# Hybrid decoder trunk on one core: residual loaded into the sum's tiles, mLSTM tiles in stages, S5 output products tied behind a later product

## The chip, the cores and the metric

The kernel runs on one core of a Trainium2 chip. The metric is the device time of one execution in microseconds, from the start to the end on the chip; each kernel is run several times, and the median is compared. A core has the engines TensorE (PE, matmuls; its weight loads are listed apart as PEld), VectorE (DVE), ScalarE (ACT), GpSimd (POOL) and SyncE (SP), which here only issues DMAs. Each engine and each DMA queue works through its own list of instructions in order and waits where a semaphore tells it to.

## The reference

One layer of a recurrent decoder trunk, run for a prompt of 2048 tokens with 16 learned meta tokens ahead of it, and for 8 sample sequences of 8 tokens. D_MODEL is 1024; three branches of width 512 are fed by one combined projection and gated into the sum.

```
h = rms_norm(x, norm_w)
proj = h @ w_in                        # q,k,v of two branches, S5 input, gates
qkv = causal_conv(conv_buf, dn_qkv)    # DeltaNet: short conv, l2 norms, delta rule in chunks
o_dn = rms_norm(delta_rule(q, k, v, g, beta)) * silu(dn_z)
o_ml = rms_norm(mlstm(q, k, v, ig, lf)) * sigmoid(ml_o) * silu(ml_z)   # matrix memory (c, n, m)
y5 = gelu(s5(s5_u));  y5 = y5 * sigmoid(y5 @ w_glu + b_glu);  o_s5 = y5 * silu(s5_z)
mixed = gates[0] * (o_dn @ w_branch_dn) + gates[1] * (o_ml @ w_branch_ml) + gates[2] * (o_s5 @ w_branch_s5)
x = x + mixed @ w_out
y = rms_norm(x, final_norm_w)
```

The outputs are y for both groups and all recurrent states.

## The kernel before

Tokens run in six blocks of (2, 3, 3, 3, 3, 2) tiles of 128; the first block also has the 80 sample and meta tokens. Activations stand with features on the partitions and the block's tokens T (336, then 384, at last 256) along the free dimension.

A product (`product`, `mm` at L195) is one 128 x T tile of output. fp32 is made of two halves: for each k the weight tile w (128 x 512, four k at once, 256 KB, DMA on SP's queue, L221) is cast to wh on ACT (L222) and VectorE subtracts wl = w - wh (L184), and three matmuls wh xh, wh xl, wl xh go into one of three PSUM banks named pd. Products with 8 k have 24 matmuls; those of the branch outputs (`wb`) and of `wg` have 12. Three buffers each hold wh and wl. So TensorE follows a stream of weights, ACT and VectorE prepare it, and in between they evict finished products and do the branches' own work.

What a block does is listed in a string of steps (`PLAN`, `PLAN0` for the first block): u and s are the S5 projections and scans, d and m the DeltaNet and mLSTM projections (numbers 8 to 11 are the v heads), M the mLSTM tiles (`ml_tile`), F the S5 finish, N the mLSTM output (`ml_out`, by `finish`), inv and D the DeltaNet inverse and tiles, E its output (also by `finish`), X2, X1 and X0 the gated branch sums (`mix`). After the steps come the next block's `norm` and this block's `out`. The code is recorded in that order; a scheduler in the framework then settles each engine's order from it, from priorities and from its own guesses of durations.

`norm` loads x in eight rows (xt, L329, SP's queue), sums squares (nacc, nsq), has a matmul that spreads the reciprocal root (`pr<-nsq,c`), scales xt in place on VectorE, casts it to xh on ACT (L357) and leaves xl to POOL. `out` does eight products of mh and ml with `wo`. For each it loads the residual row into a temporary ox on ACT's queue (L1320), and VectorE evicts with h = 0.5 pd + ox (L192). Then come the squares of h, the last norm, and the store of h (L1329, ACT's queue).

`ml_tile` for one tile: spread and exp (mlew, mldd), qk on TensorE, q * ew on POOL (`ml<-ml,mlew`), transposes of k and v (`tok`, `tr` at L199), kw = k * wst on VectorE, va = v on ACT (L894) with a column of ones set by POOL (L895), then the products with the state (`pr<-c,ml`) and with the tile (`pr<-va,mldd`). The DeltaNet's matrix P is scaled on POOL (`P<-P,dnx`, and `P<-P,ff` in `finish`). `s5_scan` has input products, a scan on VectorE and POOL (s5a), and output products (`s<-s5a,s5w`).

Of the kernel before, what the change touches and what calls it, by code (L numbers as in the profile page):

```python
# [38 lines left out]
PLAN0 = ("m8 m7 R m6 m10 m1 m0 m9 m2 m4 m5 d4 m3 d5 m11 M d0 d3 d2 S d7 d8 d9 d10 d1 d6 pre inv d11 N X1 D "  # L39
         "F X2 Ud E X0 Um").split()  # L40
PLAN = ("u0 u1 u2 u3 s0 s1 s2 s3 d0 d1 m1 m0 m2 m3 d6 d2 d10 d3 m4 m7 m6 d7 d4 d5 m5 d8 pre d9 m9 d11 m11 m10 m8 M F N inv D X2 "
        "X1 E X0").split()
# [10 lines left out]
    "macc": "wide", "ox": "wide", "rb": "wide", "s5v": "raw", "s5g": "wide", "raw": "raw", "junk": "junk",  # L53
# [49 lines left out]
class Kernel:  # L103
# [123 lines left out]
    def product(self, src, nk, xh, xl, T, lead=None):  # L227
# [4 lines left out]
        for k in range(nk):  # L232
# [4 lines left out]
            self.mm(o, l[:, k % 4], xh(k), start=False, stop=k == nk - 1)  # L237
# [11 lines left out]
    def setup(self):  # L249
# [41 lines left out]
        self.s_i = self.c_i = 0  # L291


    def block(self, b):
        self.b = b
# [16 lines left out]
        self.us = self.us_d[b % 2]  # L312
        self.ys = self.ys_d[b % 2]
        self.dn, self.ml, self.br, self.cst, self.acc = [None] * 3, [None] * 3, [None] * 3, None, None

        self.segs = ([(0, 8, 8), (NS, 1, NM)] if self.first else []) + [(self.p0, BLOCKS[b], P)]

    def norm(self):

        T, V = self.T, self.V  # L320
        xu = [self.unit([P, 4, T], name="xt") for _ in range(2)]
        xt = [xu[k // 4][:, k % 4] for k in range(8)]
        for k in range(8):
            src = self.I["xt"][k, :, self.t0:self.t0 + T]
            if self.first:
# [6 lines left out]
        if self.first:  # L332
# [11 lines left out]
        with self.tc.high_priority(offset=5000 if self.first else 0):  # L344
            rb = self.rstd_row(acc)
        xh, xl = ([self.xp.tile([P, 4, TMAX], F32R, name=self.name(s), tag=s, bufs=2)[:, :, :T] for _ in range(2)]
                  for s in ("xh", "xl"))
        if self.first:
            self.rb = self.temp([P, TMAX], "rb")[:, :T]
            self.A.copy(self.rb, rb)  # L350
            self.xh, self.xl, self.xn = uh, ul, (xh, xl)
        else:
            self.xh, self.xl = xh, xl
        with self.tc.high_priority(offset=3000 if self.first else 0):
            for k in range(8):
                self.stt(xt[k], xt[k], w(k), rb, OP.mult, OP.mult)
                self.A.copy(xh[k // 4][:, k % 4], xt[k])  # L357
                self.tt(V if self.first and k < 4 else self.G, xl[k // 4][:, k % 4], xt[k], xh[k // 4][:, k % 4], OP.subtract)
# [4 lines left out]
    def add_square(self, acc, x, first):  # L363
        if first:
            self.act(acc, x, AF.Square)
        else:
            sq = self.temp([P, TMAX], "nsq")[:, :self.T]
# [3 lines left out]
    def rstd_row(self, acc):  # L371

        T, V, nt = self.T, self.V, self.nt
        pc = self.ps([P, nt])
# [1150 lines left out]
```

## Time and profile before

| | us |
|---|---|
| median of three runs | 2824.74 |
| lowest and highest of the three | 2822.19, 2829.98 |
| the profiled execution, its own time | 2815.57 |
| its span, first to last instruction | 2813.8 |
| TensorE busy in the span | 2657.2 |
| TensorE's mean granted clock | 0.975 |

The profiled execution is one more execution, with the profiler on; its time lies 9.2 us below the median, and 1.8 us of it lie outside the span. Times of trace rows count from the start of the span. The granted clock is a share of full speed (2.4 GHz); 0.50 is the lower level, 1.2 GHz. A matmul's row gives the time to its modelled end; consecutive matmuls overlap, so their spacing is read from the starts.

### The profile page before, as it was taken

The numbers are of one execution on the slowest core, as the hardware profiler recorded it, in microseconds if no ns is written. First come the engines' busy times: TensorE is split into PE (matmuls) and PEld (weight loads), VectorE is DVE, ScalarE is ACT, GpSimd is POOL, SyncE is SP. The second block draws the span as 40 slices with busy tenths as digits, with TensorE's granted clock in tenths as the row PEclk, the third lists the DMA queues.
The fourth block names the chain that finished last, engine by engine and source line by source line (L and its number), as shares of the span: only waits on it lengthen the run. The fifth ranks groups of instructions, "written<-read, shape, count | busy, mean of one in ns | idle before, by whom it ended". The sixth has DMA issues, their size and how long they took to land.

```text
span 2813.8 us, 49701 instructions
## 1 busy us (share of the span) xinstructions
PE 2657.2 (94%) x17416; PEld 2579.1 (92%) x17416; DVE 2049.5 (73%) x4386; ACT 1256.8 (45%) x2855; POOL 759.0 (27%) x917
## 2 busy tenths in 40 slices
PE   6898999989999999999999999999999999988998
PEld 5898898989999989899999989999899999988998
DVE  8888766788764587885568788456888745689865
ACT  4353343534533444553344454344445434445544
POOL 7642333222302312321230241123123012113022
PEclk8998999999999999999999999999999999999999
DMA  5544546555343455433345533335554434564545
GB/s 153 164 151 143 162 137 200 181 161 158 104 123 102 140 179 159 136 109 115 107 147 169 172 118 120 107 114 156 168 162 116 130 94 126 155 201 144 174 136 154
DMA packets 303290, 404.24 MB, mean 144 GB/s; under 512 B 109472, under 2 KB 138912, under 8 KB 303040
## 3 DMA queue, kind: packets, MB, share of 16 engines
q1 hardware_dynamic: 283248, 374.73, 44.6%
q10 hardware_dynamic: 19792, 26.34, 2.8%
q8 instruction: 137, 2.24, 0.3%
q14 instruction: 113, 0.93, 0.1%
HBM read 369.42 MB, written 31.53 MB: 142 GB/s over the span
## 4 chain that ended last, share of the span: by engine, by line
PE 80%; DVE 11%; POOL 3%; DMA 2%; issue 2%; ACT 1%; SPq 0%; DVEq 0%; ACTq 0%; POOLq 0%
PE pd L195 66%; PE pr L195 9%; PE s L195 3%; DVE wl L184 2%; PE pr L199 2%; DVE s5a L1205 1%; POOL s5a L184 1%; DMA ox<-in_xt_dram 1%; DVE h L192 1%; DVE s5a L184 1%; DVE cacc L192 1%; DMA w<-in_wi_dram 1%; POOL P L184 1%; POOL s5xy L184 0%; ACT xh L357 0%
## 5 line engine op out<-in xcount | busy, mean ns | idle before, releaser
L222 ACT CAST wh<-w 128x512 fp32r<-128x512 f32 x1092 | 673.9, 619 | 990.5 <-PE pd L195 828.5
L184 DVE TENSOR_TENSOR wl<-w,wh 128x512 fp32r<-128x512 f32 x1092 | 812.7, 746 | 407.1 <-ACT wh L222 393.4
L195 PE MATMUL pd<-xh,wh 128*128 128x384 f32 (+2 forms) x3272 | 1078.7, 330 | 28.5 <-DVE cacc L192 16.8
L195 PE MATMUL pd<-xh,wl 128*128 128x384 f32 (+2 forms) x3272 | 1078.7, 330 | 17.5 <-DVE wl L184 17.0
L195 PE MATMUL pd<-xl,wh 128*128 128x384 f32 (+2 forms) x3272 | 1070.4, 327 | 9.4 <-DVE xl L184 9.4
L195 PEld LDWEIGHTS pd<-xh,wh 128*128 128x128 f32 x3272 | 625.5, 191 | 36.0 <-issue 8.4
L195 PEld LDWEIGHTS pd<-xh,wl 128*128 128x128 f32 x3272 | 624.4, 191 | 34.1 <-DVE wl L184 28.3
L195 PEld LDWEIGHTS pd<-xl,wh 128*128 128x128 f32 x3272 | 625.7, 191 | 11.8 <-DVE xl L184 9.8
L184 POOL TENSOR_TENSOR macc<-macc,mt 128x384 f32<-128x384 f32 (+2 forms) x96 | 124.7, 1299 | 389.0 <-DVE mt L192 382.3
L184 POOL TENSOR_TENSOR s5a<-s5a,s5a 128x384 f32<-128x384 f32 (+2 forms) x72 | 76.9, 1075 | 555.4 <-DVE s5a L184 522.6
L195 PE MATMUL pd<-mh,wh 128*128 128x384 f32 (+2 forms) x384 | 126.5, 331 | 11.6 <-ACT xh L357 7.0
L195 PE MATMUL pd<-mh,wl 128*128 128x384 f32 (+2 forms) x384 | 126.3, 331 | 3.9 <-DVE wl L184 3.6
L195 PE MATMUL pd<-ml,wh 128*128 128x384 f32 (+2 forms) x384 | 125.9, 329 | 0.0
L192 DVE SCALAR_TENSOR_TENSOR cacc<-pd,c,cacc 128x384 f32<-128x384 f32 (+1 forms) x180 | 103.9, 582 | 2.8 <-ACT cacc L181 1.5
L192 DVE SCALAR_TENSOR_TENSOR mt<-mt,pd 128x384 f32<-128x384 f32 (+2 forms) x96 | 50.1, 522 | 73.5 <-PE pd L195 73.1
L195 PE MATMUL s<-s5U,s5w 128*128 128x96 f32 (+2 forms) x576 | 86.0, 278 | 14.9 <-issue 9.2
L178 POOL COPY U<-UC 32x128 f32<-32x128 f32 x68 | 21.7, 337 | 290.5 <-DMA UC<-scru 289.2
L195 PEld LDWEIGHTS s<-s5U,s5w 128*128 128x128 f32 x576 | 79.3, 197 | 16.0 <-issue 15.5
L184 POOL TENSOR_TENSOR s5a<-s5a,s5t 128x384 f32<-128x384 f32 (+2 forms) x48 | 69.5, 1447 | 72.7 <-issue 32.7
L195 PEld LDWEIGHTS pd<-mh,wh 128*128 128x128 f32 x384 | 74.2, 193 | 14.6 <-ACT xh L357 13.0
L181 ACT ACTIVATE mt<-pd,c 128x384 f32<-128x384 f32 (+2 forms) x144 | 79.4, 551 | 0.4
L195 PEld LDWEIGHTS pd<-mh,wl 128*128 128x128 f32 x384 | 74.2, 193 | 5.9 <-DVE wl L184 5.8
(399 smaller groups left out, 4476.5 us busy)
## 6 DMA issues: line engine op xcount, KB each, us to landing
w<-in_wi_dram SPq DMA_DIRECT2D x816, 256.0 KB
w<-in_wb_dram SPq DMA_DIRECT2D x144, 256.0 KB
s5w<-s5w SPq DMA_DIRECT2D x120, 256.0 KB
w<-in_wo_dram SPq DMA_DIRECT2D x96, 256.0 KB
s5t<-s5p SPq DMA_DIRECT2D x48, 192.0 KB
w<-in_wg_dram SPq DMA_DIRECT2D x24, 256.0 KB
xt<-in_xt_dram SPq DMA_DIRECT2D x32, 192.0 KB
ox<-in_xt_dram ACTq DMA_DIRECT2D x32, 192.0 KB
```

Source lines behind the costliest of these rows:

```text
L178: return eng.tensor_copy(out, in_)
L181: return self.A.activation(out, in_, f, **k)
L184: return eng.tensor_tensor(out, a, b, op=op)
L192: return self.V.scalar_tensor_tensor(out, a, s, b, op0=op0, op1=op1)
L195: return self.E.matmul(out, lhsT, rhs, start=start, stop=stop, **k)
L199: return self.E.transpose(out, in_, self.ident[:n, :n])
L222: self.A.copy(h, w)
L1205: V.tensor_tensor_scan(g[:, a, 1:1 + m], self.s5R[:, 4 * f + a:4 * f + a + 1].to_broadcast([P, m]), x[:, a, 0:m], g[:, a, 0:1], OP.mult, O ...
```

## The change

There are five edits.

1. `out` allots its two tiles h (128 x 4 x T each) first and loads the residual straight into them with two DMAs on SP's queue; the eviction works in place. The temporaries ox and their eight loads on ACT's queue go.
2. Steps are generators that can be advanced by stages: a plan word `w:n` runs n stages of it, the bare word the rest. `ml_tile` has stages (spread to q * ew; kw and a small copy ec; v copy and its ones column; the products). `M0:2` stands ahead of m11 and `M1:2` ahead of m10, so that two tiles' first stages are recorded ahead of the last v projections (m11, m10, m8). The ones column is copied on ACT from a constant, and C * ec reads the small copy.
3. In the S5 scans the output products are a second stage; a word with `!` is tied by `issue_after` behind the last matmul of the product recorded last, without a semaphore. They are recorded after the next scan's input stage and two projections.
4. `finish` records the gate of head h ahead of the transposes of head h - 1.
5. `norm`, `out`, the DeltaNet tiles and `dn_pre` are written as generators too; `OUT` has all stages of norm ahead of those of out, as before, and the merge `dn_merge` is a step g of its own ahead of each D.

```diff
-PLAN = ("u0 u1 u2 u3 s0 s1 s2 s3 d0 d1 m1 m0 m2 m3 d6 d2 d10 d3 m4 m7 m6 d7 d4 d5 m5 d8 pre d9 m9 d11 m11 m10 m8 M F N inv D X2 "
-        "X1 E X0").split()
+OUT0 = ["n"] * 19 + ["o"] * 99
+PLAN = ("R C u0 u1 u2 u3 s0:1 s1:1 d0 d1 s0! s2:1 m1 m0 s1! s3:1 m2 m3 s2! d6 d2 s3! d10 d3 m4 m7 m6 d7 d4 d5 m5 d8 p d9 m9 "
+        "d11 M0:2 m11 M1:2 m10 m8 M0 M1 M2 F N I g0 D0 g1 D1 g2 D2 X2 X1 E X0").split()
+OUT = ["n"] * 19 + ["o"] * 99
...
-            self.mm(o, l[:, k % 4], xh(k), start=False, stop=k == nk - 1)
+            self.tail = self.mm(o, l[:, k % 4], xh(k), start=False, stop=k == nk - 1).ins
...
-        for h in range(4):
-            z = gate(h)
-            p = self.ps([P, T])
-            for i, (o, n) in enumerate(self.tiles):
-                self.tr(p[:, o:o + n], raw[:n, i, h])
+        z = [None] * 4
+        for h in range(5):
+            yield
+            if h < 4:
+                z[h] = gate(h)
+            if h:
+                p = self.ps([P, T])
+                for i, (o, n) in enumerate(self.tiles):
+                    self.tr(p[:, o:o + n], raw[:n, i, h - 1])
...
         self.tt(G, q[:, :, o:o + n], q[:, :, o:o + n], ew, OP.mult)
+        yield
...
         self.tt(V, kw[:n], self.tok(k, o, n), self.b4(self.wst, i, n), OP.mult)
+            ec = self.small([P, 4, 1], "mlec")
+            A.copy(ec, ew[:, :, n - 1:n])
+        yield
         A.copy(va[:n, :, 0:P], self.tok(v, o, n))
-        G.memset(va[:n, :, P:P + 1], 1.0)
+        A.copy(va[:n, :, P:P + 1], self.ones[:n, 0:4][:, :, None])
+        yield
...
-            self.tt(G, Cn, C, ew[:, :, n - 1:n].to_broadcast([P, 4, 129]), OP.mult)
+            self.tt(G, Cn, C, ec.to_broadcast([P, 4, 129]), OP.mult)
...
                     self.tt(V, x, x, y, op)
                     self.tt(V, out[j], x, bv[j][:, :, :, l], OP.add)
+        yield
         yp = self.ps([P, 4, n], "s5")
...
-    def out(self):
-        V, A, G, T = self.V, self.A, self.G, self.T
+    def out(self, g, mh, ml):
+        V, A, G, T = self.V, self.A, self.G, g.T
+
         hu = [self.unit([P, 4, T], name="h") for _ in range(2)]
+        for k in range(2):
+            self.nc.sync.dma_start(hu[k], self.I["xt"][4 * k:4 * k + 4, :, g.t0:g.t0 + T].rearrange("k p t -> p k t"))
         acc = self.temp([P, TMAX], "nacc")[:, :T]
         for d in range(8):
-            x = self.temp([P, TMAX], "ox")[:, :T]
-            self.nc.scalar.dma_start(x, self.I["xt"][d, :, self.t0:self.t0 + T])
             h = hu[d // 4][:, d % 4]
             with self.tc.high_priority(offset=WPRIO):
-                self.stt(h, ps, 0.5, x, OP.mult, OP.add)
+                self.stt(h, ps, 0.5, h, OP.mult, OP.add)
...
+            for w in PLAN0 if self.first else PLAN:
+                late = w[-1] == "!"
+                w, _, n = w.rstrip("!").partition(":")
+                if w[0] in "gMD" and int(w[1:]) >= self.nt:
+                    continue
+                with self.tc.issue_after(self.tail) if late else nullcontext():
+                    self.advance(w, steps, int(n) if n else -1)
```

How the edits move instructions is seen in the order that the scheduler makes. The first place is VectorE in the output stage of the fourth block. Names: wl is a weight's lower half, rs_t, nr and nsq are norm's reciprocal roots, xt norm's rows, h the sum's tile, pd a finished product, ox a residual row. Before:

```order
L184 TENSOR_TENSOR wl_21689<-w_21687,wh_21688 128x512
L192 SCALAR_TENSOR_TENSOR rs_t_21492<-nr_21489 128x3
L184 TENSOR_TENSOR rs_t_21492<-rs_t_21492,nvar_21488 128x3
L192 SCALAR_TENSOR_TENSOR nr_21489<-rs_t_21492,nr_21489 128x3
L188 TENSOR_SCALAR nsq_21504<-c_92,nr_21489 128x128 x3
L184 TENSOR_TENSOR wl_21714<-w_21712,wh_21713 128x512
L192 SCALAR_TENSOR_TENSOR xt_21451<-xt_21451,c_91,pr_21508 128x384 x3
L192 SCALAR_TENSOR_TENSOR h_21538<-pd_21541,ox_21578 128x384
L192 SCALAR_TENSOR_TENSOR xt_21451<-xt_21451,c_91,pr_21508 128x384
L192 SCALAR_TENSOR_TENSOR xt_21452<-xt_21452,c_91,pr_21508 128x384 x4
```

The same place of the changed kernel, with the start of norm's chain:

```order
L188 TENSOR_TENSOR wl_21606<-w_21604,wh_21605 128x512
L196 SCALAR_TENSOR_TENSOR h_21518<-pd_21523,h_21518 128x384
L188 TENSOR_TENSOR wl_21624<-w_21622,wh_21623 128x512
L196 SCALAR_TENSOR_TENSOR h_21518<-pd_21562,h_21518 128x384
L188 TENSOR_TENSOR wl_21647<-w_21645,wh_21646 128x512
L193 TENSOR_SCALAR nvar_21468<-pr_21464 128x3
```

And its end:

```order
L192 TENSOR_SCALAR nsq_21484<-c_92,nr_21469 128x128 x3
L196 SCALAR_TENSOR_TENSOR h_21518<-pd_21603,h_21518 128x384
L188 TENSOR_TENSOR wl_21688<-w_21686,wh_21687 128x512
L188 TENSOR_TENSOR nacc_21522<-nacc_21522,nsq_21600 128x384
L188 TENSOR_TENSOR nacc_21522<-nacc_21522,nsq_21641 128x384
L188 TENSOR_TENSOR wl_21706<-w_21704,wh_21705 128x512
L196 SCALAR_TENSOR_TENSOR xt_21431<-xt_21431,c_91,pr_21488 128x384 x3
L196 SCALAR_TENSOR_TENSOR h_21518<-pd_21644,h_21518 128x384
```

The first eviction stood behind the chain and behind three rows of xt; now two evictions stand ahead of the chain, the third behind nsq, and the fourth behind three rows of xt. On TensorE `pr<-nsq,c` stood at the end of the third product of `wo` and stands near the end of the fourth. On SP's queue the two loads of h follow norm's loads and stand among the first weights of `wo`: one h, a weight, the other h.

The second place is POOL around the mLSTM tiles of the fourth block. P and dn are the DeltaNet's, c_119 and c_120 the mLSTM state, ml q, s5g the S5 finish. Before:

```order
L184 TENSOR_TENSOR c_120<-c_119,mlew_18498 128x516
L184 TENSOR_TENSOR s5g_18689<-s5g_18689,s5g_18685 128x384
L184 TENSOR_TENSOR P_18121<-P_18121,dnx_18213 128x512 x3
L184 TENSOR_TENSOR s5g_18702<-s5g_18702,s5g_18698 128x384
L184 TENSOR_TENSOR ml_17756<-ml_17756,mlew_18498 128x4x128
L895 MEMSET va_18578 128x4
```

Now:

```order
L188 TENSOR_TENSOR c_120<-c_119,mlec_18383 128x516
L188 TENSOR_TENSOR ml_17730<-ml_17730,mlew_18358 128x4x128
L188 TENSOR_TENSOR s5g_18669<-s5g_18669,s5g_18665 128x384
L188 TENSOR_TENSOR ml_17730<-ml_17730,mlew_18425 128x4x128
L188 TENSOR_TENSOR s5g_18682<-s5g_18682,s5g_18678 128x384
L188 TENSOR_TENSOR P_18095<-P_18095,dnx_18187 128x512 x3
```

The q products of two tiles went ahead of the three P, and the memset is gone.

The third place is TensorE at the same tiles, at the end of the last v projection (pd); va is v with its ones, mldd the weights in the tile. Before:

```order
L195 MATMUL pd_18457<-xh_16316,wl_18478 128x384
L195 MATMUL pr_18508<-ml_17756,ml_17413 128x128 x4
L199 MATMUL pr_18517<-c_92,ml_17413 128x128 x4
L199 MATMUL pr_18523<-c_92,ml_18295 128x128 x4
L195 MATMUL pr_18531<-c_119,ml_17756 128x129
L195 MATMUL pr_18531<-va_18516,mldd_18502 128x129
```

Now:

```order
L199 MATMUL pd_18490<-xh_16304,wl_18511 128x384
L203 MATMUL pr_18528<-c_92,ml_18269 128x128 x4
L199 MATMUL pr_18536<-c_119,ml_17730 128x129
L199 MATMUL pr_18543<-c_119,ml_17730 128x129
L199 MATMUL pr_18536<-va_18376,mldd_18362 128x129
```

qk and the transposes of k (the first two rows behind pd before) went ahead, into the projections before this one; the transposes of v stay. Elsewhere on TensorE the S5 output products stand in whole groups of twelve inside later products, and the transposes of the DeltaNet's finish stand 18 matmuls ahead of the first branch product, where they stood 55 ahead.

## Rows read from the trace of the kernel before

**Rows 1.** The page, busy time of each engine and the chain that ended last

```profile
PE 2657.2 (94%) x17416; PEld 2579.1 (92%) x17416; DVE 2049.5 (73%) x4386; ACT 1256.8 (45%) x2855; POOL 759.0 (27%) x917
...
PE 80%; DVE 11%; POOL 3%; DMA 2%; issue 2%; ACT 1%; SPq 0%; DVEq 0%; ACTq 0%; POOLq 0%
```

**Rows 2.** Windows, one steady block: busy us (x count), granted clock, DMA share, GB/s

```profile
1930.00:2405.00 475.00, 459.71 (x2902) 450.82 (x2901) 337.24 (x698) 212.22 (x476) 111.15 (x110) 0.99 0.45 135
```

**Rows 3.** TensorE's waits: us in total, times, longest us

```profile
PE pd L195 <- DVE wl L184: 21.6, 28, 2.7
...
PE pr L195 <- POOL va L895: 15.4, 3, 5.2
...
PE s L195 <- POOL s5a L184: 8.3, 5, 2.5
...
PE pr L195 <- DVE nsq L188: 6.9, 6, 3.1
...
PE pr L195 <- POOL ml L184: 3.2, 1, 3.2
```

**Rows 4.** Timeline of TensorE, two output stages: start us, us, instruction, idle before

```profile
1943.27 0.33 PE L195 MATMUL pd<-mh,wh 128*128 128x384 f32 x1
1943.44 0.33 PE L195 MATMUL pd<-ml,wh 128*128 128x384 f32 x1
...
1944.47 0.88 PE L195 MATMUL pr<-nsq,c 128*128 128x384 f32 x2 [0.52 <-DVE nsq L188]
1947.67 0.51 PE L195 MATMUL pd<-mh,wh 128*128 128x384 f32 x1 [2.32 <-ACT xh L357]
...
2423.70 0.66 PE L195 MATMUL pd<-mh,wh 128*128 128x384 f32 x1 [3.95 <-DVE h L192]
```

**Rows 5.** Timeline of VectorE, the first of these stages

```profile
1945.40 1.66 DVE L192 SCALAR_TENSOR_TENSOR xt<-xt,c,pr 128x384 f32<-128x384 f32 x3 [0.24 <-PE pr L195]
1946.98 0.55 DVE L192 SCALAR_TENSOR_TENSOR h<-pd,ox 128x384 f32<-128x384 f32 x1
```

**Rows 6.** Timeline of ACT and its queue (ACTq), the same stage

```profile
1924.42 0.62 ACT L222 CAST wh<-w 128x512 fp32r<-128x512 f32 x1 [0.98 <-PE pd L195]
...
1943.82 0.83 ACTq L1320 DMA_DIRECT2D ox<-in_xt_dram  x2
```

**Rows 7.** Windows after five waits, and one of the loads ahead

```profile
1947.70:1951.70 4.00, 4.00 (x14) 4.00 (x15) 3.41 (x7) 3.66 (x8) 4.00 (x5) 0.57 0.03 3
2423.70:2430.00 6.30, 6.30 (x22) 6.30 (x23) 2.95 (x5) 2.02 (x4) 3.02 (x4) 0.57 0.22 63
1661.80:1668.20 6.40, 6.39 (x27) 6.39 (x28) 3.38 (x10) 3.86 (x14) 1.25 (x2) 0.52 0.40 121
711.30:716.50 5.20, 5.15 (x27) 5.15 (x28) 2.62 (x8) 3.69 (x14) 1.25 (x2) 0.67 0.40 102
2579.50:2583.50 4.00, 3.98 (x21) 3.98 (x22) 2.84 (x12) 2.25 (x10) 1.57 (x2) 0.60 0.41 123
1915.00:1925.00 10.00, 10.00 (x60) 10.00 (x59) 5.01 (x7) 5.14 (x10) 3.26 (x3) 1.00 0.86 272
```

**Rows 8.** Timeline of TensorE at the mLSTM tiles of one block

```profile
1661.81 0.80 PE L195 MATMUL pr<-c,ml 128*128 128x129 f32 x2 [5.15 <-POOL va L895]
```

**Rows 9.** Timeline of POOL at the same tiles

```profile
1655.14 3.68 POOL L184 TENSOR_TENSOR P<-P,dnx 128x512 f32<-128x512 f32 x3 [2.99 <-DVE dnx L184]
...
1661.70 0.10 POOL L895 MEMSET va<- 128x4 f32 x1
```

**Rows 10.** Timelines of ACT and of VectorE at the same tiles

```profile
1659.76 0.57 ACT L894 COPY va<-pr 128x512 f32<-128x512 f32 x1
...
1661.16 0.67 DVE L184 TENSOR_TENSOR kw<-pr,cx 128x512 f32<-128x512 f32 x1
```

**Rows 11.** Timeline of SP's queue ahead of the output stage

```profile
1918.69 0.91 SPq L329 DMA_DIRECT2D xt<-in_xt_dram  x2
1919.70 14.47 SPq L221 DMA_DIRECT2D w<-in_wo_dram  x7
```

**Rows 12.** Timelines of POOL and TensorE at the DeltaNet's finish

```profile
1869.34 3.94 POOL L184 TENSOR_TENSOR P<-P,ff 128x512 f32<-128x512 f32 x3 [6.85 <-DVE ff L192]
...
1873.96 0.38 PE L199 MATMUL pr<-c,P 128*128 128x128 f32 x2
```

**Rows 13.** Timeline of TensorE at the mLSTM tiles of the last block

```profile
2576.77 0.66 PE L199 MATMUL pr<-c,ml 128*128 128x128 f32 x4 [0.87 <-ACT ml L181]
...
2579.52 0.80 PE L195 MATMUL pr<-va,mldd 128*128 128x129 f32 x2 [1.65 <-ACT va L894]
```

More of the change, by code (lines that the diff above doesn't have):

```diff
@@ L1 @@
 import math
-from contextlib import ExitStack
+from contextlib import ExitStack, nullcontext
+from types import SimpleNamespace
 import numpy as np
@@ L712, in tok, with state @@
         return t
+    def state(self, s, i):
+        k = max(sum(BLOCKS[:self.b]) + i - self.first, 0)
+        return s[k % 2], s[(k + 1) % 2]
     def b4(self, t, i, n):
@@ L919, in ml_tile @@
             self.act(junk[:n], self.mraw[:n, i, h], AF.Square, accum_out=self.mss[:n, i, h:h + 1])
[L920 to L922 removed]
+        yield
         for a in range(2):
@@ new lines, in steps @@
+        self.U = [None] * self.nt
+        out = {"R": (self.rows,), "C": (self.columns,), "p": (self.dn_pre,), "I": (self.dn_inv,), "N": (self.ml_out,),
+               "E": (self.dn_out,), "F": (self.s5_finish,), "S": (self.s5_setup_low,), "norm": (self.normed,),
+               "Um": (self.ml_samples_out,), "Ud": (self.dn_samples_out,)}
+        for n in range(12):
+            out["d%d" % n] = self.dn_proj, kqv[n]
+            out["m%d" % n] = self.ml_proj, kqv[n]
+        for f in range(4):
+            out["u%d" % f] = self.s5_proj, f
+            out["s%d" % f] = self.s5_scan, f
@@ L1379, in plan, with advance @@
+        for i in range(self.nt):
+            out["M%d" % i] = self.ml_tile, i
+            out["g%d" % i] = self.dn_merge, i
+            out["D%d" % i] = self.dn_tile, i
+        return out
+    def advance(self, w, steps, n):
+        if w not in self.live:
             if w[0] == "X":
-                add(self.mix, int(w[1]), self.mixed == 0, self.mixed == 2)
+                self.live[w] = self.mix(int(w[1:]), self.mixed == 0, self.mixed == 2)
                 self.mixed += 1
-        return out
+            else:
+                f, *a = steps[w]
+                self.live[w] = f(*a) or iter(())
+        while n and next(self.live[w], self) is not self:
+            n -= 1
@@ L1396, in run @@
         self.setup()
+        out = iter(())
         for b in range(len(BLOCKS)):
@@ L1399, in run @@
             self.scr_p, self.scr_u = scr_p[b % 2], scr_u[b % 2]
-            if b == 0:
-                self.norm()
+            if self.first:
+                for _ in self.norm(self.shape(0)):
+                    pass
                 self.s5_powers()
@@ L1407, in run @@
                     self.G.memset(t, 1.0)
[L1408 to L1420 removed]
+            steps, self.live, self.mixed = self.steps(), {"O": out}, 0
+            for w in PLAN0 if self.first else PLAN:
[5 more added lines that the diff above has]
+                    self.advance(w, steps, int(n) if n else -1)
+            for w in self.live:
+                self.advance(w, steps, -1)
+            out = self.out(self.shape(b), self.mh, self.ml_)
+            norm = iter(()) if self.last else self.norm(self.shape(b + 1))
+            for w in OUT0 if self.first else OUT:
+                next(out if w == "o" else norm, None)
+            if self.last:
+                for _ in out:
+                    pass
+            else:
+                self.xh, self.xl = self.xn
         nc, O = self.nc, self.O
[L1422 to L1423 removed]
+        nc.scalar.dma_start(O["p_dns"], self.S[sum(BLOCKS) % 2])
+        nc.scalar.dma_start(O["p_mlc"], self.C[sum(BLOCKS) % 2])
 _SHAPES = {
```

222 lines of the change are left out of this document (94 added, 128 removed).

## Prediction

> **What bounds the kernel now.** I read the page first. TensorE is busy for 94% of the span and carries 80% of the chain that ended last; VectorE's part of that chain is 11% [rows 1]. The change neither adds nor removes a product, so it can only win time in which TensorE waits, or in which it runs at a lower granted clock just after a wait. The windows say how much of that there is: a steady block of 475 us has 459.71 us of busy TensorE, so some 15 us of waiting, at a mean granted clock of 0.99 [rows 2]. The list of TensorE's waits names them [rows 3]. Next I read the timeline around the three places the change touches.
>
> *The output stage.* After the third product of `out` TensorE computes the next norm's row of reciprocal roots (`pr<-nsq,c`) and then stands for 2.32 us ahead of the fourth product [rows 4]. The list puts this down to the cast of xh, which the waiting matmul doesn't read. What it needs is one of the three PSUM banks: all three hold finished products, and the first eviction (`h<-pd,ox`) runs at 1946.98 us on VectorE, behind three rows of norm (`xt<-xt,c,pr` x3, 1.66 us), ending at 1947.53 [rows 5]. The eviction could not have come much earlier anyway, since its residual tile was only issued at 1943.82 on ACT's queue [rows 6]. For 4.0 us after the wait the granted clock averages 0.57, mostly its lower level (1.2 instead of 2.4 GHz), which costs another 4.0 x 0.43 = 1.7 us [rows 7]. The same wait of 2.32 stands in three blocks; in the fifth output stage it is 3.95 us, and the clock after it 0.57 over 6.3 us, 2.7 us more [rows 4, 7].
>
> *The mLSTM tiles.* When the last v product is done TensorE does qk and two sets of transposes of tile 0 and then stands 5.15 us [rows 8]. At that time three engines hold it up: POOL does three `P<-P,dnx` (3.68 us) first and reaches the `va` memset at 1661.70 [rows 9]; VectorE's kw ends at 1661.83 and ACT's copy of v at 1660.33 [rows 10]. Over the next 6.4 us the clock is 0.52: 3.1 us more [rows 7]. Three blocks have this wait (15.4 us together) and one has 3.2 us for POOL's q product [rows 3], with 5.2 us at 0.67 after it, 1.7 us [rows 7].
>
> *S5.* TensorE reaches output products of a scan before POOL's sums are there: 8.3 us at five places, 2.5 at most [rows 3].
>
> **The change part by part.** All sums are made against the profiled execution, 2815.6 us. The median of the runs shown is 2824.7, 9.1 higher; I carry the difference over to that median unchanged.
>
> *Residual in the sum's tiles.* In the changed order two evictions stand ahead of norm's whole chain on VectorE and the third right behind nsq, and the row of roots stands nearly one product (24 matmuls) later on TensorE. So the bank is free when the fourth product comes, and VectorE has some 4 us more (24 matmuls at the 0.17 us that lie between the two starts ahead of the wait [rows 4]) for the chain. What can go: 3 x (2.32 + 1.7) = 12.1; 3.95 + 2.7 = 6.7; and the waits for nsq, 6.9 less 3.1 for the longest, which is the final one after the last product and stays: 3.8 [rows 3]. Together 22.5. I take **-20**, since the fourth eviction still follows three rows of norm, and a half microsecond may stay at each. Bounds: 0 and -22.5. The 48 issues that leave ACT (two take 0.83 us [rows 6]) count nothing besides: ACT is busy for 45% of the span [rows 1], and what waited for their data is in the sum.
>
> *What that costs.* The two loads (2 x 128 x 4 x 384 x 4 bytes = 1.57 MB) go on SP's queue, behind norm's eight rows and around the first two weights of `wo`. In the 10 us in which norm's rows and weights pass now, the engines move 272 GB/s at a share of 0.86 [rows 7]; at that rate 1.57 MB take 5.8 us. The first weight of `wo` is issued at 1919.70 [rows 11] and cast at 1924.42, where the cast waited for TensorE and not for the load [rows 6]: 4.7 us for a transfer of 0.26 MB, 1 us at that rate. The first weight has half of the new bytes ahead of it and keeps its time (1 + 2.9 = 3.9); the second has all, but is needed one weight, 2.1 us, later. So it is nearly hidden. Bounds: 0, and at the other end the full 5.8 us of delay with the 1.7 us of slow clock, 7.5 in each of six output stages, 45. I take **+5**, nearer to 0 because the cast shows slack. The loads' tiles are freed by the DeltaNet tiles' last matmuls and by the transposes ahead of the branch products, of which one runs at 1873.96 now [rows 12], some 45 us before the issue, so SP doesn't wait for them.
>
> The Trainium skill, DMA: Bandwidth & Descriptors, section Queues, rings and completion order, has a rule that speaks against this part: each DMA engine takes one row's descriptors in ring order and changes between rows by turns. The residual stood in ACT's row, where it only shared turns with the weights; by the rule it now stands ahead of them. By the rule alone the second weight is late by an estimated 5.8 us less its slack, and the sum would move towards the dearer bound; the row of the cast speaks for the slack, and no run here has yet shown such a burst.
>
> *mLSTM tiles in stages.* The spread, exp, qk, q product, kw and transposes of k of tiles 0 and 1 go into the two products ahead of m8. POOL has the first tiles' q products ahead of the three P, the memset is gone, and kw is done early. Behind m8 there remain the transposes of v, ACT's copy of it and the matmuls. The nearest price for that is the last block of before, where POOL and VectorE were not late: TensorE waits 0.87 and 1.65 us for ACT alone, and 4.0 us at 0.60 follow, 1.6 us [rows 13, 7]; 4.1 in all. Now: 15.4 + 3 x 3.1 + 3.2 + 1.7 = 29.6. After: 4 x 4.1 = 16.4. So **-13**. Bounds: -29.6 if the copy is hidden too; -4.4 if ACT's copy stays where it is (it ended at 1660.33, 1.48 ahead of the 1661.81 at which TensorE went on, in three blocks). The two small copies that a tile adds on ACT lie in its idle half [rows 1].
>
> *S5 output products behind a later product.* With a whole product between sums and use, the waits of 8.3 should go; **-7**. Bounds 0 and -8.3. The work moves to places where VectorE is fuller: TensorE now waits 21.6 us at 28 places for wl [rows 3]. S5's scans, pushed together, may lengthen these. I take a quarter more, **+5**; bounds 0 and a doubling, +21.6.
>
> *Finish with the gate ahead.* The DeltaNet transposes come nearer to the first branch product: 18 matmuls (3.1 us) instead of 55 (9.5 us) ahead of it. Today POOL ends `P<-P,ff` at 1873.28 and the transposes follow at 1873.96 [rows 12], so the chain has 0.7 us of slack, and merges and tiles moved later by 36 matmuls (6.2 us) push POOL too. Bounds 0 and 3 us in each of five blocks, 15; the first branch product needs one head at first, so **+3**.
>
> Sum: -20 + 5 - 13 - 7 + 5 + 3 = **-27**. Profiled 2789, on the median's footing **2798**.
>
> **The rivals.** *All waits go and nothing is paid* (-22.5 - 29.6 - 8.3 = -60): 2764. For it: every engine but TensorE has a quarter of its time free in a block [rows 2]. Against it: ACT's copy of v has to come between m8 and the matmuls in any order.
>
> *The mLSTM wait stays, with ACT's copy as its end* (-20 - 4.4 - 7 + 13 = -18): 2806. For it: the copy ended only 1.5 us before the wait did. Against it: before that copy ACT stood waiting, so an earlier S5 clears the way.
>
> *The output stage gives back what it wins:* TensorE reaches the next block's first products 20 us earlier in sum and waits there for VectorE, which still has norm's rows, evictions and squares to do: net -7, 2818, no difference that the measurement can tell. It decides if VectorE is full between the fourth `wo` product and d0; in the slow 4.0 us it is busy for 3.41 [rows 7], but a steady block leaves it a quarter idle.
>
> *Slower:* the burst of 1.57 MB on SP's queue makes the `wo` weights late. At 7.5 us in six stages, 45 in place of 5, the sum is -27 + 40 = +13: 2838. It decides from 5.3 us a stage on (27 / 6 + 5 / 6), and shows as slower from 6.8. Against it stands the slack of 4.7 us at the cast.
>
> **How the numbers follow.** Forecast 0.50, all gains 0.16, mLSTM wait stays 0.10, given back 0.13, slower 0.11. Runs of this kernel spread over 7.8 us, about 0.3%, which is the least that counts as a difference. Faster: 0.50 + 0.16 + 0.10 = 0.76; same 0.13; slower 0.11. The range goes from 2762, just past the case of all gains, to 2826, past the case given back and short of the slower one; it leaves out the 0.11 and a little on the low side.
>
> **What would show it.** In the changed kernel's profile: no wait of over 1 us ahead of the fourth `wo` product, and the clock at 1.00 there; the wait in the mLSTM stage near 2.5 us, ended by ACT and not by POOL; no wait for s5a of 2 us; wl waits near 27 us in sum. Wrong would be: casts of `wo` weights that wait for the load; a wait for `P` or `fin` ahead of the first branch product; or products after the output stage that wait for wl where none waited before.

## The result and the profile after

| | before | changed |
|---|---|---|
| median, us (four runs each) | 2825.07 | 2775.94 |
| lowest and highest, us | 2822.19, 2829.98 | 2773.69, 2777.80 |
| the profiled execution, us | 2815.57 | 2773.69 |
| span, us | 2813.8 | 2771.9 |

The profiled execution of the changed kernel is the fastest of its four runs; that of the kernel before is one more run, which the four don't hold. The ratio is 0.9824, with a 95% interval of 0.9807 to 0.9841: 49 us less by the medians, 42 by the profiled executions. The forecast was 27 less, 2798, with a range from 2762 to 2826. The direction and the range were right, and the size was little more than half.

The page of the changed kernel, engines and chain, answers to [rows 1]:

```profile
PE 2643.5 (95%) x17416; PEld 2567.8 (93%) x17416; DVE 2052.8 (74%) x4386; ACT 1259.3 (45%) x2888; POOL 787.7 (28%) x900
...
PE 78%; DVE 11%; POOL 3%; DMA 3%; issue 3%; ACT 2%; SPq 0%; ACTq 0%; DVEq 0%; POOLq 0%
```

TensorE's busy time fell by 13.7 us with the same number of matmuls, of which the mean granted clock (0.978 against 0.975 over the span) accounts for an estimated 9 (2813.8 x 0.025 - 2771.9 x 0.022); the other 28 of the 42 are time in which TensorE stood idle and no longer does. Its list of waits (us in total, times, longest) answers to [rows 3]:

```profile
PE pr L203 <- ACT ml L185: 17.1, 5, 3.9
PE pd L199 <- DVE wl L188: 13.7, 24, 2.7
PE pd L199 <- ACT wh L226: 13.2, 14, 2.1
...
PE pr L199 <- DVE nsq L192: 3.1, 1, 3.1
...
PE pd L199 <- ACT xh L367: 2.3, 1, 2.3
...
PE s L199 <- POOL s5a L188: 1.2, 1, 1.2
```

No row names `va` on POOL any more, and the waits for h are gone. The 3.1 for nsq is the last norm's, behind the last product. In place of POOL's 15.4 and 3.2 us stand 17.1 us for ACT's eviction of the last v projection, and the casts of weights (wh) have 13.2 us, where they had 4.5 before: what wl lost, wh gained, and the two together are 26.9 against 26.1.

In the output stage of the fourth block VectorE now evicts two products ahead of norm's chain, which answers to [rows 5] (timeline: start us, us, instruction):

```profile
1913.73 0.55 DVE L196 SCALAR_TENSOR_TENSOR h<-pd,h 128x384 f32<-128x384 f32 x1
...
1914.80 0.55 DVE L196 SCALAR_TENSOR_TENSOR h<-pd,h 128x384 f32<-128x384 f32 x1
...
1915.86 0.16 DVE L193 TENSOR_SCALAR nvar<-pr 128x3 f32<-128x3 f32 x1
```

TensorE goes from the third product into the fourth at its fast spacing, without the wait of [rows 4] (timeline):

```profile
1918.79 0.34 PE L199 MATMUL pd<-mh,wl 128*128 128x384 f32 x1
1918.97 0.33 PE L199 MATMUL pd<-mh,wh 128*128 128x384 f32 x1
```

The window over the 4 us from there (columns as in [rows 2]) has the clock at 1.00, where [rows 7] has 0.57:

```profile
1918.90:1922.90 4.00, 4.00 (x25) 4.00 (x24) 3.44 (x8) 2.20 (x4) 0.00 (x0) 1.00 0.43 127
```

Both kernels do the same products in each block in nearly the same order, so the start of a product in one trace can be set against its start in the other. The fourth `wo` product, for one, starts at 1947.67 before and at 1918.97 now, 28.7 us earlier; the first one of that stage started 25.7 us earlier. Taken at the ends of four stages, in us that the stage became longer (+) or shorter:

| stage | forecast | block 0 | 1 | 2 | 3 | 4 | 5 | sum |
|---|---|---|---|---|---|---|---|---|
| up to the projection d7 (the first two S5 scans) | -7 + 5 | | -7.4 | -0.3 | -0.1 | +0.7 | +5.4 | -1.7 |
| d7 to the first mLSTM gate product (the last two S5 scans, mLSTM tiles, S5 finish) | -13 | | -1.3 | -3.0 | -5.5 | -5.4 | -6.7 | -21.9 |
| from there to `wo` (DeltaNet, branch sums) | +3 | | +0.1 | +0.2 | +0.2 | +0.2 | +1.8 | +2.5 |
| output stage | -20 + 5 | -2.9 | -5.0 | -4.9 | -3.6 | -7.3 | -0.4 | -24.1 |
| block 0 up to its output stage | 0 | +4.2 | | | | | | +4.2 |

The last block's output stage is taken to its last product; the norm behind that is 0.9 us shorter too. The cut at d7 doesn't part S5 from the mLSTM tiles: in blocks 1 to 4 of both kernels the output products of the third and fourth scan stand behind d7 and ahead of m11, the first of the last three v projections. In blocks 2 to 4 sixteen S5 input matmuls, 1.7 us, also went from behind d7 to ahead of it. A cut at m11 does part them. In blocks 1 to 4 the stretch up to m11 is 7.5, 3.6, 2.7 and 2.6 us shorter, and the one from m11 to the gate product changes by -1.2, +0.3, -2.8 and -2.1. So of the 22 us that these four blocks won ahead of the gate product, 16.4 lie in the stretch of the S5 scans and 5.8 in that of the mLSTM tiles.

### The profile page after: what moved, and what is told of

Its sections match the earlier page's. It is cut to its first block, busy times and chain, and to the rows that moved or that the text cites. A ratio compares the mean times of both kernels' runs of the same rounds, so it can differ in the third digit from the quotient of the medians.

```text
span 2771.9 us, 49619 instructions
## 1 busy us (share of the span) xinstructions
PE 2643.5 (95%) x17416; PEld 2567.8 (93%) x17416; DVE 2052.8 (74%) x4386; ACT 1259.3 (45%) x2888; POOL 787.7 (28%) x900
## 4 chain that ended last, share of the span: by engine, by line
PE 78%; DVE 11%; POOL 3%; DMA 3%; issue 3%; ACT 2%; SPq 0%; ACTq 0%; DVEq 0%; POOLq 0%
PE pd L199 64%; PE pr L199 9%; PE s L199 3%; DVE wl L188 2%; PE pr L203 2%; DVE cacc L196 1%; POOL s5a L188 1%; DVE s5a L1243 1%; POOL s5xy L188 1%; ACT wh L226 1%; DVE h L196 1%; DVE s5a L188 1%; DMA w<-in_wo_dram 1%; POOL s5t L188 0%; DMA w<-in_wi_dram 0%
## 5 line engine op out<-in xcount | busy, mean ns | idle before, releaser
L188 DVE TENSOR_TENSOR wl<-w,wh 128x512 fp32r<-128x512 f32 x1092 | 829.6, 762 | 386.5 <-ACT wh L226 378.9
L188 POOL TENSOR_TENSOR s5a<-s5a,s5t 128x384 f32<-128x384 f32 (+2 forms) x48 | 82.6, 1721 | 98.5 <-DVE s5a L1243 53.4
L1243 DVE TENSOR_TENSOR_SCAN s5a<-s5R,s5a,s5a 128x96 f32<-128x96 f32 (+2 forms) x192 | 74.1, 443 | 18.2 <-ACT s5a L1241 16.7
```

Of the source, the lines that this page charges most:

```text
L188: return eng.tensor_tensor(out, a, b, op=op)
L1243: V.tensor_tensor_scan(g[:, a, 1:1 + m], self.s5R[:, 4 * f + a:4 * f + a + 1].to_broadcast([P, m]), x[:, a, 0:m], g[:, a, 0:1], OP.mult, O ...
```

## The experiments

Each run's ratio stands against the kernel before on the same chip, with its 95% interval; "us" is that ratio's distance from 1 times 2825. The changed kernel is at -50 by that measure. An interval is 4 to 7 us to each side of a single value, so two kernels some 6 us apart or less aren't told apart. Stages compare one profiled execution of each kernel.

**The residual alone, and the rest without it.** The first is the kernel before with this edit:

```diff
         hu = [self.unit([P, 4, T], name="h") for _ in range(2)]
+        for k in range(2):
+            self.nc.sync.dma_start(hu[k], self.I["xt"][4 * k:4 * k + 4, :, self.t0:self.t0 + T].rearrange("k p t -> p k t"))
...
-            x = self.temp([P, TMAX], "ox")[:, :T]
-            self.nc.scalar.dma_start(x, self.I["xt"][d, :, self.t0:self.t0 + T])
...
-                self.stt(h, ps, 0.5, x, OP.mult, OP.add)
+                self.stt(h, ps, 0.5, h, OP.mult, OP.add)
```

> The kernel before with one edit: the residual goes into the sum's tiles by two DMAs on SP's queue, evicted in place. Theory (the first eviction waited for its residual and for norm's rows, and the gain stays): the waits ahead of the fourth product of the output stage go, and with them the slow clock; 24 us less than before in sum over the six output stages, 2801 us against 2825. Rival 1 (the next block's first products give it back): under 8 us less, 2817 or more. Rival 2 (the load's burst on SP's queue makes the weights of the output product late): slower than before, casts there wait for the load.

Measured: 2799.5, ratio 0.9910 (0.9897 to 0.9924), -25 us. The second is the changed kernel with the same edit reversed:

> The changed kernel with the residual back in temporaries that ACT's queue loads, all else as changed. Theory: the output stage's gain hangs on this edit alone, so 24 us more than the changed kernel, 2800 us, with waits of 2.3 us ahead of the fourth product again. Rival (norm and output written as stages move the evictions forward by themselves): within 5 us of the changed kernel's 2776.

Measured: 2802.1, ratio 0.9925 (0.9912 to 0.9937), -21 us, 29 behind the changed kernel. Its list of TensorE's waits has the old entries again:

```profile
PE pd L199 <- ACT xh L367: 9.5, 4, 2.6
...
PE pd L199 <- DVE h L196: 4.8, 2, 4.0
```

So this edit gives 25 to 29 us whether the others are there or not, and within the intervals it is independent of them. It does two things at once, it brings the residual earlier and lets the evictions stand earlier in VectorE's order; no run parts the two. Writing norm and output as stages moves nothing by itself: in the trace of this second kernel the first eviction runs behind three rows of norm as it did before.

**mLSTM stages and S5 stages, each undone and both.** In the changed kernel's plan:

```diff
 # mLSTM not early
-"d11 M0:2 m11 M1:2 m10 m8 M0 M1 M2 ..."
+"d11 m11 m10 m8 M0 M1 M2 ..."
 # S5 whole
-"... s0:1 s1:1 d0 d1 s0! s2:1 m1 m0 s1! s3:1 m2 m3 s2! d6 d2 s3! d10 ..."
+"... s0 s1 s2 s3 d0 d1 m1 m0 m2 m3 d6 d2 d10 ..."
```

> The changed kernel with all stages of the mLSTM tiles behind the last v projection; the column of ones still comes from ACT and the decay from the small copy. Theory (the early stages win the time): 20 us more than the changed kernel, 2796, and the wait behind the last v projection is 5 us again. Rival (it was POOL's memset behind the three P, which is still gone here): within 6 us of 2776.

> The changed kernel with each S5 scan in one piece, in the order of before, no tie. Theory (the stage's waits went but its twelve products cost as much elsewhere, and block 1 alone won 7 us while the last block lost 5): within 5 us of 2776, the waits for s5a back at 2.5 us in three blocks. Rival (the S5 edit is worth the 7 us that it was forecast to remove): 2783.

> The changed kernel with both undone: S5 scans in one piece and all mLSTM stages behind the last v projection (residual, finish, column of ones as changed). Theory (the two edits overlap: an S5 that is finished earlier takes the work off ACT, VectorE and POOL that held up the mLSTM tiles, so either edit alone clears most of the same wait): clearly more than the sum of the two single losses, 13 + 5, over the changed kernel: 2799 or more, near the residual alone (2799.5). Rival (the two add): 2776 + 18 = 2794.

Measured, as us against before (medians in brackets):

| | mLSTM early | mLSTM behind v |
|---|---|---|
| S5 in stages | -50 (2775.9, the changed kernel) | -44 (2780.8; 0.9844, 0.9830 to 0.9857) |
| S5 whole | -35 (2789.2; 0.9877, 0.9864 to 0.9891) | -17 (2806.9; 0.9939, 0.9926 to 0.9951) |

Against the corner without either, S5 alone gives 27, mLSTM alone 17, and both give 33, not 44. Two of my theories fell. The early mLSTM stages are worth 6 us and not 20, and since the two intervals overlap, not even the 6 are shown. S5, which I held to be even, is worth 15, with the intervals apart.

Where the 15 lie is seen when the kernel with S5 whole is set beside the changed one. Up to m11 it is 7.3, 3.7, 4.5 and 2.9 us longer in blocks 1 to 4; from m11 to the gate product it is 0.4 to 1.5 us shorter. (In the last block its scans run past m11, so the cut doesn't part them there.) So with the mLSTM stages early the gain lies in the stretch of the scans themselves, and no wait for POOL at the tiles has part in it. Its list of TensorE's waits has 9.9 us for s5a and 18.7 for wl, where the changed kernel has 1.2 and 13.7.

The other 12 us, which S5 is worth only where the mLSTM stages are late, come from one wait ahead of the products with the state, which the list of the corner without either names:

```profile
PE pr L199 <- POOL ml L188: 18.3, 4, 5.0
```

None of the other three corners has such a row: the two edits clear the same wait, and the traces show how. POOL at the tiles of the fourth block with S5 in stages and mLSTM not early (timeline):

```profile
1633.28 3.67 POOL L188 TENSOR_TENSOR P<-P,dnx 128x512 f32<-128x512 f32 x3 [0.32 <-DVE dnx L188]
1636.91 1.72 POOL L188 TENSOR_TENSOR ml<-ml,mlew 128x512 f32<-128x512 f32 x1
```

TensorE in the same kernel, the first transposes behind the last v projection and the first product with the state:

```profile
1637.57 0.60 PE L203 MATMUL pr<-c,ml 128*128 128x128 f32 x4
...
1639.18 0.39 PE L199 MATMUL pr<-c,ml 128*128 128x129 f32 x2
```

POOL with both undone:

```profile
1650.12 4.47 POOL L188 TENSOR_TENSOR P<-P,dnx 128x512 f32<-128x512 f32 x3 [2.86 <-DVE dnx L188]
...
1655.95 1.26 POOL L188 TENSOR_TENSOR ml<-ml,mlew 128x512 f32<-128x512 f32 x1
```

TensorE there:

```profile
1651.12 1.12 PE L203 MATMUL pr<-c,ml 128*128 128x128 f32 x8
1657.26 0.80 PE L199 MATMUL pr<-c,ml 128*128 128x129 f32 x2 [5.02 <-POOL ml L188]
```

In both, POOL does the three P first and the q product behind them. With S5 in stages VectorE has dnx ready 4.3 us ahead of the transposes (1637.57 - 1633.28), so the q product ends at 1638.63, ahead of the product with the state that needs it (1639.18). With S5 whole dnx is 1.0 us ahead (1651.12 - 1650.12), the q product ends at 1657.21, and TensorE waits 5.02 us. This is block 3 of the table. Blocks 1, 2 and 4 are alike: 4.3 us ahead with S5 in stages, and with it whole 1.1 us ahead in two and 1.1 behind in block 1. The dnx are sooner because the scans ahead of them on VectorE end sooner: in the block shown, counted from its start, VectorE ends its last s5a at 123.6 us instead of 141.5 and its last dnx at 153.0 instead of 160.0. The early mLSTM stages reach the same end by another way: they put the q product ahead of the three P. The memset that [rows 9] shows last is no part of it: it is gone in all four corners, and the residual alone, which still has it, waits as long (19.7 us at four places, put down to va) as the corner without either (18.3).

With mLSTM not early the mLSTM stage itself is 2 to 4 us shorter than in the changed kernel in blocks 1 to 4. But the DeltaNet's last tile then stands 11 matmuls later among the products. Ahead of and in the first product of X0 TensorE waits 0.53, 0.57 and 0.19 us for zt and dnl, the clock over the 6 us there is 0.72, and from the first gate product to `wo` blocks 1 to 3 take 3.6 us more and block 4 takes 2.1. That eats the difference.

By the scheduler's order the `!` ties do nothing here: without them the order is the same, row for row, on all five engines. No run shows it.

**The finish.**

```diff
-        for h in range(5):
-            yield
-            if h < 4:
-                z[h] = gate(h)
-            if h:
...
+        for h in range(4):
+            yield
+            z = gate(h)
```

> The changed kernel with the gate of each head recorded right ahead of its own transposes, as before. By the order, the DeltaNet tiles then stand 36 matmuls earlier again. Theory (the edit only moves work about; by stages it was even): within 4 us of 2776. The forecast's term (it costs 3 us): 2773. Rival (it holds the rest of the gain that the other edits leave open, some 5 us): 2781.

Measured: 2778.9, ratio 0.9843 (0.9828 to 0.9857), -44 us; its interval overlaps the changed kernel's. The DeltaNet tiles do stand some 36 matmuls earlier, and each of its blocks is within 2 us of the changed kernel's, but for 3 us in block 0. The edit is worth nothing to 5 us; the forecast's cost isn't shown.

**The residual's load.** The changed kernel with the two loads issued twice, and with them on ACT's queue:

```diff
 # twice
+        for k in range(2):
+            self.nc.sync.dma_start(hu[k], self.I["xt"][4 * k:4 * k + 4, :, g.t0:g.t0 + T].rearrange("k p t -> p k t"))
 # ACT's queue
-            self.nc.sync.dma_start(hu[k], self.I["xt"]...
+            self.nc.scalar.dma_start(hu[k], self.I["xt"]...
```

> The changed kernel with the residual loaded twice into the same tiles, so 3.1 instead of 1.6 MB stand ahead of and among the first weights of the output product. Theory (weights in the same queue come behind it; one load made the second weight's cast wait 2.2 us, of which three weight buffers left 0.5 us to TensorE): the casts wait some 6 us in each of six stages and TensorE 3 to 5 with a slow clock after it, 2796 to 2812. Rival (the transfers share turns and the weights aren't late): within 5 us of 2776.

> The changed kernel with the two residual loads issued from ACT's queue instead of SP's, into the same tiles. Theory (on SP's queue the weights of the output product stand behind the residual; on a queue of its own it only shares turns): no cast of the first weights waits 2.2 us for its load, and TensorE's 0.5 to 1.2 us in each stage go, 2 to 4 us less than 2776. Rival (at a DMA share of 1.03 the engines are full, so weights are as late from either queue): 2776 within 3, with the casts' waits still there.

Measured: twice 2772.0, ratio 0.9833 (0.9814 to 0.9851), -47 us; ACT's queue 2775.7, ratio 0.9823 (0.9805 to 0.9840), -50 us. Neither differs from the changed kernel, though the casts do wait. ACT in the changed kernel (timeline):

```profile
1904.67 0.62 ACT L226 CAST wh<-w 128x512 fp32r<-128x512 f32 x1 [2.17 <-DMA w<-in_wo_dram]
```

Windows of 5 us over the burst in the same kernel:

```profile
1895.00:1900.00 5.00, 5.00 (x31) 5.00 (x30) 2.76 (x4) 2.60 (x5) 1.36 (x2) 1.00 1.03 365
1900.00:1905.00 5.00, 5.00 (x31) 5.00 (x30) 0.88 (x2) 1.47 (x3) 2.06 (x2) 1.00 1.04 368
```

TensorE, at the end of that, and VectorE just before it:

```profile
1909.65 0.45 PE L199 MATMUL pd<-mh,wl 128*128 128x384 f32 x1 [0.54 <-DVE wl L188]
```

```profile
1907.15 1.84 DVE L188 TENSOR_TENSOR nacc<-nacc,nsq 128x384 f32<-128x384 f32 x2
1908.92 0.68 DVE L188 TENSOR_TENSOR wl<-w,wh 128x512 fp32r<-128x512 f32 x1
```

For 10 us the engines are full at 365 GB/s, and the second weight's cast waits 2.17 us for its load. At most 0.54 of it reaches TensorE: that wait is for the third weight's wl, which on VectorE stands behind two of norm's sums, and in blocks 1, 2 and 4, whose casts wait 1.56 to 2.03 us, TensorE has no wait over 0.1 us in the first two products. Only block 0 has more, 1.19 us for a cast that waited 0.61. The rest is covered by the weights already cast. ACT's waits for weights in the run with the loads twice (us in total, times, longest):

```profile
ACT wh L226 <- DMA w<-in_wo_dram: 19.6, 12, 2.2
```

SP's queue in the same run (list of its waits):

```profile
SPq L1364 <- DMA h<-in_xt_dram: 24.5, 12, 4.2
```

And in the run with them on ACT's queue:

```profile
ACT wh L226 <- DMA w<-in_wb_dram: 14.1, 6, 3.4
...
ACT wh L226 <- DMA w<-in_wo_dram: 5.6, 6, 2.0
```

The changed kernel has 11.1 us at 8 places for `wo` in ACT's list and 1.1 at one place for `wb`. The run with the loads twice isn't the burst of double length that its expectation describes: each second load waits in SP's queue until the first has landed in the same tile, so that in the fourth block the two are issued behind three and four weights of `wo`, 7 and 8 us later than the first loads. The waits of the casts nearly double in sum, but none is longer than 2.2 us, and the time stays. What a longer burst ahead of the second weight would cost is not shown. On ACT's queue the waits move from `wo` to the branch weights (`wb`) that are on the way at that time. The Trainium skill, DMA: Bandwidth & Descriptors, section Queues, rings and completion order, says that descriptors of one row are taken in ring order and rows by turns. The trace agrees as to which weight is late: behind the residual on one queue (`wo`, 11.1 us), beside it on two (`wb`, 14.1 us). The time is the same within the intervals.

**What is left of the mLSTM wait.** In the changed kernel TensorE stands 3.30 us ahead of the transposes of v (timeline):

```profile
1638.12 1.12 PE L203 MATMUL pr<-c,ml 128*128 128x128 f32 x4 [3.30 <-ACT ml L185]
```

The clock over the 3.9 us after it is 0.61 (window; the second row is the window behind the wait of 3.31 us in block 2):

```profile
1638.10:1642.00 3.90, 3.88 (x21) 3.77 (x22) 1.93 (x5) 1.74 (x5) 1.38 (x1) 0.61 0.21 34
1170.80:1177.00 6.20, 6.20 (x29) 6.09 (x30) 3.07 (x8) 3.90 (x14) 1.38 (x1) 0.51 0.48 128
```

ACT in that time:

```profile
1636.64 0.52 ACT L185 ACTIVATE s5g<-s5g 128x384 f32<-128x384 f32 x1 [2.09 <-DVE s5g L196]
...
1637.58 0.48 ACT L185 ACTIVATE ml<-pd 128x384 f32<-128x384 f32 x1
```

The v projection ended at 1634.8, but its eviction stands on ACT behind a square of the S5 finish that waits 2.09 us for VectorE. Three ways were tried to take that wait away. The first gives TensorE tile 1's first stages as cover:

```diff
-"d11 M0:2 m11 M1:2 m10 m8 M0 M1 M2 ..."
+"d11 M0:2 m11 m10 m8 M1:2 M0 M1 M2 ..."
```

> The changed kernel with only tile 0's first stages early, and tile 1's recorded behind the last v projection. In its order eight transposes and three other matmuls stand where the changed kernel has four transposes, ahead of the products with the state. Theory (with both tiles early TensorE has nothing to do while ACT finishes the last v product, hence the new 3.3 us wait for ACT): the wait falls to about 2 us in each of five blocks and the DeltaNet order stays as changed, 2766 to 2771. Rival (the wait only moves behind the transposes, to the copy of v): 2776 within 4.

Measured: 2784.0, ratio 0.9859 (0.9845 to 0.9874), -40 us: worse. The theory fell. TensorE's waits have moved to VectorE's work for the tiles:

```profile
PE pr L199 <- DVE mldd L188: 7.9, 4, 2.1
...
PE pr L199 <- DVE kw L188: 4.9, 5, 1.1
```

The second ties the order on ACT (vact is the eviction of v):

```diff
-            self.act(t, yf, AF.Square)
+            with self.tc.issue_after(self.vact) if f == 2 and not self.first else nullcontext():
+                self.act(t, yf, AF.Square)
```

> The changed kernel with one order tied on ACT: the third S5 finish square is queued behind the eviction of the last v projection (no other engine's work is touched by hand). In the changed kernel ACT reaches that square first, waits 2.1 us for VectorE in it, and only then evicts v, for which TensorE stands 3.3 us. Theory (that order on ACT is what is left of the mLSTM wait): the wait falls to about 1 us in four or five blocks and the slow clock after it mostly goes, 10 to 18 us less than the changed kernel's 2776. Rival 1 (VectorE's mldd or kw, or the copy of v, ends the wait as late): 2776 within 4. Rival 2 (the S5 finish is late for its gate products instead): 2776 or more, with a new wait ahead of them.

Measured: 2774.5, ratio 0.9820 (0.9802 to 0.9837), -51 us: no difference. The wait for v falls to 0.9 us, and the second rival holds; the gate product behind waits for the S5 finish instead (list of TensorE's waits):

```profile
PE pd L199 <- ACT yh L1310: 7.8, 6, 2.0
...
PE pr L199 <- ACT va L937: 5.4, 5, 2.1
PE pr L203 <- ACT ml L185: 4.6, 5, 0.9
```

The third records the first S5 gate projection ahead of the first gate product, so that 24 matmuls which need nothing from ACT come behind the v projection:

```diff
+            z = None if f or self.first else self.silu2(CB_S5Z + f)
             ps = self.product(self.I["wg"][f], 4, lambda k: yh[:, k], lambda k: yl[:, k], T)
...
-            z = self.silu2(CB_S5Z + f)
+            z = z if z is not None else self.silu2(CB_S5Z + f)
```

> The changed kernel with the first S5 gate projection recorded ahead of the first gate product (blocks after the first). In its order the 24 matmuls of that projection stand between the last v projection and the transposes of v, where the changed kernel waits 3.3 us for ACT. Theory (TensorE only lacks work that needs nothing from ACT there): the 3.3 us wait and the slow clock after it go in four blocks, and no wait for the first gate product's input takes their place, since it comes as late as before; 10 to 16 us less than 2776. Rival (the tiles' work comes one product later, and the gate products then wait for yh or the next steps for the tiles): 2776 within 4.

> As the run with the S5 gate projection as cover, and with v's eviction tied ahead of the third S5 square on ACT as in the earlier run. Theory (with a product as cover ACT's order no longer matters): the same time as the cover alone within 3 us, some 2763. Rival (both are needed: v's eviction still comes after the cover ends): 5 us or more below the cover alone.

Measured: the cover 2760.8, ratio 0.9766 (0.9741 to 0.9791), -66 us, and with ACT's order tied too 2765.5, ratio 0.9781 (0.9759 to 0.9804), -62 us, the same within the intervals. The cover beats the changed kernel by some 16 us, and in its trace what is left at the place is the copy of v (TensorE's timeline):

```profile
1631.35 0.49 PE L199 MATMUL pr<-va,mldd 128*128 128x129 f32 x2 [0.84 <-ACT va L935]
```

The window around it has the clock at 1.00:

```profile
1629.40:1633.60 4.20, 3.36 (x30) 3.14 (x29) 2.72 (x5) 2.88 (x8) 0.35 (x1) 1.00 0.57 156
```

## Why the prediction was right, and where its size was off

*The output stage: right, and mis-sized by its cost.* The cause was read rightly: the bank that the fourth product needs, held by an eviction behind norm's rows and without its residual, not the cast that the list names. Which of these two weighs more is open, since one edit takes both away. The term was -20 + 5; the stage measured -24.1, and the edit alone -25. The step that was off is the load's cost of 5: at most 0.54 us reaches TensorE in the stage shown, 1.19 in block 0's and nothing over 0.1 in the first two products of the others. The sign named for it appeared (casts that wait for the load), but it didn't decide. The term of -20 was also short of what the waits and the clock gave, 22.5 by its own bound; some 3 us of waits for wl late in two of the stages went besides, which it hadn't counted.

*The mLSTM tiles: right about the new wait, too dear in its gain.* The forecast was that POOL's wait would go and one for ACT stay, 4.1 us a block with the slow clock. The waits that stayed are 3.30 or 3.31 in blocks 1 to 4, and the clock after them cost 1.7, 3.0, 1.5 and 1.7 more (0.56 over 3.9 us, 0.51 over 6.2, 0.61 over 3.9, 0.72 over 6.2): 21.1 in all and 5.3 a block. Before it was 29.6 by the forecast and 27.5 by the trace, because the slow clock of 3.1 us, read in one block, was taken for three; the other two have 1.5 and 2.6 (0.77 and 0.60 over 6.4 us). So the waits gained 6.4 in place of 13, as the stretch from m11 (5.8) and the run that undoes the early stages (6) say too. With S5 in stages alone the wait for POOL is gone already.

*The S5 output products: the gain was right, the hand-back had the wrong sign, and a wait further on was left out.* The waits for s5a fell from 8.3 to 1.2, as forecast. The term was -7 + 5; the run with S5 whole is 15 us slower than the changed kernel. In its list s5a has 8.7 us more and wl 5.0 more, so the scans in stages didn't lengthen the waits for wl, as the +5 had it, they shortened them; these two rows, 13.7 us, are the largest that grew (the wait for ACT at the tiles is 4.7 less), and how the 15 add up from all of them stays open. And where the mLSTM stages are late the edit is worth 27, because VectorE then has dnx ready some 3 us sooner against TensorE and POOL's q product is done in time. The prediction priced the edit where it stands and looked only for what it might cost later.

*The finish.* +3 was forecast, +2.5 stood in the stages, 1.8 of it in the last block; the run that undoes it can't tell it from nothing.

*The footing.* I carried the 9.1 us between the profiled execution of before and its median over to the changed kernel. There it is 2.3, since the profiled execution is the fastest of the four runs, so 7 of the 22 us by which the forecast fell short of the medians lie outside any term.

Left open: block 0's 4.2 us up to its output stage; its waits for loads and issues differ between runs of kernels that don't touch it, from 5 us less to 3 more than the changed kernel. Also open is why the corner without S5 and mLSTM edits (-17) lies 8 us behind the residual alone (-25), when the finish and the other small edits are all that tells them apart; the profiled executions of the two show 2.5 us of it.

## What to carry to other kernels

Before pricing an edit where it stands, follow its engine's queue on to the next wait on the path: here scans that ended 18 us earlier on VectorE let POOL start on P 7 us earlier, some 30 us further on, and two edits that clear one wait didn't add up. Before giving a stage's gain to an edit, see which work the cut really holds: here half of the scans stood behind it. The wait put down to an eviction was best covered by a product that needs nothing from the waiting engine; reordering that engine's own queue only handed the wait to the next in line. And a burst of loads costs what the buffers behind it don't cover, so the wait of a cast isn't yet one of TensorE. A second load into a tile that a load is still filling waits for it, so it doesn't make the burst longer.

## What the runs showed of the hardware

Waits of like length cost different sums by the clock after them. In the changed kernel 3.30 us is followed by 3.9 us at 0.61 in block 3, 1.5 us more, and 3.31 at the same place of block 2 by 6.2 us at 0.51, 3.0 more. Before the change 2.32 us in the output stage had been followed by 0.57 over 4.0 us [rows 7]; yet a wait of 2.44 us for s5a in block 2 was followed by a clock of 1.00, and so were those of 2.46 and 2.47 in blocks 3 and 4 (timeline, and the window behind it):

```profile
1078.28 0.46 PE L195 MATMUL s<-s5a,s5w 128*128 128x96 f32 x2 [2.44 <-POOL s5a L184]
```

```profile
1078.30:1084.30 6.00, 6.00 (x41) 6.00 (x42) 2.50 (x4) 3.10 (x9) 0.00 (x0) 1.00 0.65 198
```

In the same block 2.01 us for cacc was followed by 6.0 us at 0.72. The run with the gate projection as cover, which waits 0.84 us at the mLSTM tiles, stays at 1.00 too. So the length of a wait alone doesn't tell what the clock adds; what else decides it is not shown here.
